# Hybrid decoder layer: another order of the output product's pieces, and a later place for one weight split

## The chip, the cores and the metric

The kernel runs on one core of one Trainium2 chip. The metric is the device time of one execution in microseconds (us); for the kernel before the change it is 1205.36 us, the median of 3 runs (1204.99 to 1206.16).

Engine names are those of the profile: PE (matrix products; PEld is its weight load), DVE (elementwise), ACT (activation functions, copies), POOL and SP (here they only issue transfers). Each engine has one queue of instructions, whose order is fixed when the program is built.

## What is computed

One decoder layer over 512 tokens of width 1024, in float32: a SwiGLU feed-forward block (ffn1), a mixer that joins dilated attention and a gated recurrence, and a second SwiGLU block (ffn2). The change lies where the mixer ends and ffn2 begins:

```python
merged = gates[:, :, 0] * attn_d + gates[:, :, 1] * rec_d
h = h + rms_norm(merged @ w_out[l], mix_norm_post[l])

f = swiglu(rms_norm(h, ffn2_norm_pre[l]), ffn2_w_gate[l], ffn2_w_up[l], ffn2_w_down[l])
h = h + 0.5 * rms_norm(f, ffn2_norm_post[l])
```

## The kernel before

**Number format.** A product of two float32 matrices is made of three: each operand is split into a high part (a copy rounded to the format that PE takes, made by ACT) and a low part (the rest, a subtraction on DVE). `split` (L317, L318) does it for weights; they come from memory over SP's queue into four `raw` buffers (L254), and a buffer is free again when the subtraction has read it. Lines L446 to L448 and L330 to L332 are the three products, high by high, high by low, low by high.

**Tokens in blocks.** The 512 tokens are four blocks of 128. `merged @ w_out` has rows = tokens and 1024 columns, taken as two halves of 512. The half of the contraction that comes first (`merged` columns 0 to 511) is done ahead of the change with a scheme of seven block products; its sums for every block and half lie in `facc`. The other half of the contraction is done by `out_product` (L537) in **eight pieces**, one for each (half, block): four steps over the contraction, three products each, twelve products of 128x512. Its weights are the four tiles `wo[0]` to `wo[3]`: the first two for half 0, the last two for half 1, two contraction steps in each. They are split by `other(0)` to `other(3)`, and the last of them is the only one named `wo` in the profile; the other three are named `act`.

**A piece** begins with a seed: ACT copies the earlier sum from `facc` into one of five PSUM accumulators (`begin`, L545). PE adds the twelve products. ACT squares the result and sums the squares along the row (`square`, L439, into `sq`); DVE multiplies by the norm's gain into `facc` (L554). A seed of a later piece waits until the accumulator of five pieces earlier has been read by L554.

**A block** is closed by `Boundary.block` behind the piece with its half 1. It needs the sums of squares of both halves. `root` (L426 to L433) makes the norm's factor in five small DVE steps with one ACT step (L428) between; DVE then adds the scaled block to the residual `h` (L572, two halves), ACT squares `h` (L439), POOL sends `h` to memory (`kept`, L574), a second `root` follows for the norm that ffn2 begins with, and DVE makes `u` (L579, two halves). The two `u` of a block are held until `Boundary.turn` takes them.

**A turn** transposes a block for ffn2: for each half four PE transposes into one of three `aux` PSUM buffers (L588), ACT's copy of the high part (L592), DVE's low part (L593) into `xf`, and ACT's copy of the whole into `facc` (L594).

**What follows.** `gemm_first` does the first five weight matrices of ffn2, first for tokens 0 to 255 (blocks 0 and 1), then for 256 to 511, with products of 128x256 (L330 to L332). Blocks 2 and 3 are turned behind the third and fourth matrix of the first round. Four of the five weight matrices have ordinary buffers (`w`); the fifth goes into `tx`. Its split is traced inside `issue_after` of two instructions named by `bd2.done[1]`: on ACT and on DVE it is queued behind them.

**Order.** The kernel's text gives a priority: what is written earlier goes first, unless it is not ready by the builder's estimate; `high_priority(offset)` moves instructions up (AHEAD for weight splits, EVAC for `root`). The builder writes out each engine's queue from that.

Of the kernel before, what the change touches and what calls it, by code (L numbers as in the profile page):

```python
# [10 lines left out]
F32 = mybir.dt.float32  # L11
F32R = mybir.dt.float32r
AF = mybir.ActivationFunctionType
ALU = mybir.AluOpType
# [172 lines left out]
def hybrid_layer(ctx: ExitStack, tc: tile.TileContext, xT: bass.AP, xN: bass.AP, wst: bass.AP,  # L187
                 first: bass.AP, rows: bass.AP, consts: bass.AP, bias: bass.AP, out: bass.AP):
    nc = tc.nc
    DVE, ACT, PE = nc.vector, nc.scalar, nc.tensor  # L190
# [25 lines left out]
    def hb(b, sl=slice(0, D)):  # L216

        return hs["t"][b // 2].rearrange("p k t -> p (k t)")[:, b % 2 * D:b % 2 * D + D][:, sl]

    def fb(b, sl=slice(0, D)):  # L220
        return facc[:, 2 * b:2 * b + 2, :].rearrange("p k t -> p (k t)")[:, sl]
# [14 lines left out]
    state = {"g": 0, "i": 0, "off": 0, "raw": None, "ahead": AHEAD, "split": None}  # L236
# [83 lines left out]
    def acc_ps():  # L320
        return psum.tile([P, T], F32, name="acc", tag="acc", bufs=5)

    def aux_ps():
        return psum.tile([P, T], F32, name="aux", tag="aux", bufs=3)

    def tmp(name):
        return tpool.tile([P, T], F32, name=name, tag="t")
# [84 lines left out]
    def stat():  # L412
        return tpool.tile([P, 1], F32, name="stat", tag="stat", bufs=24)

    def root(sums, f, then=lambda: None):


        *firsts, last = sums
        c = -0.5 * f / D
        with tc.high_priority(offset=EVAC):  # L420
            s0, bias_, y, v, r = (stat() for _ in range(5))
            s = firsts[0]
            if len(firsts) > 1:
                s = stat()
                DVE.tensor_add(s, *firsts)
            DVE.tensor_scalar(bias_, s, 1.0 / D, EPS, op0=ALU.mult, op1=ALU.add)  # L426
            DVE.tensor_scalar(s0, s, D * EPS, c, op0=ALU.add, op1=ALU.mult)
            ACT.activation(y, last, AF.Abs_reciprocal_sqrt, bias=bias_, scale=1.0 / D)  # L428
            with_last = DVE.scalar_tensor_tensor(v, last, c, s0, op0=ALU.mult, op1=ALU.add).ins
            with tc.issue_after(with_last):  # L430
                then()
            DVE.scalar_tensor_tensor(v, v, y, y, op0=ALU.mult, op1=ALU.mult)
            DVE.scalar_tensor_tensor(r, v, 1.5 * f, y, op0=ALU.add, op1=ALU.mult)  # L433
        return r

    def square(src):

        q, t = tmp("sq"), stat()
        state["square"] = ACT.activation(q[:, :src.shape[-1]], src, AF.Square, accum_out=t).ins  # L439
        return t  # L440

    def tokens(ps, ws, x, b, fill=lambda: None, ks=None, cs=slice(0, T), seeded=False):
        bl = slice(b * P, (b + 1) * P)
        for k in ks or range(x.n):
            wh, wl = (w.rearrange("p (k c) -> p k c", k=2)[:, k % 2, cs] for w in ws[k // 2])
            PE.matmul(ps, x.hi[k][:, bl], wh, start=k == 0 and not seeded, stop=False, skip_group_check=True)  # L446
            PE.matmul(ps, x.hi[k][:, bl], wl, start=False, stop=False, skip_group_check=True)  # L447
            PE.matmul(ps, x.lo[k][:, bl], wh, start=False, stop=k == x.n - 1, skip_group_check=True)  # L448
            if k == x.n // 2 - 1:
                fill()  # L450
# [7 lines left out]
    FHALVES = (slice(0, T), slice(T, D))  # L458

    def gains(pool, *ids):  # L460
# [5 lines left out]
        return t[:, 0, :], t[:, 1, :]  # L466

    def last_product(key, nk, x, added, grow, slots, block, fills={}, apart=False):


# [23 lines left out]
        def out_of(ps, b, cs, z=None):  # L494
            src, y = ps, fb(b, cs)
            if added and not apart:
                DVE.tensor_add(y, src, y)
                src = y
            sums.setdefault(b, []).append(square(src))
            return lambda: DVE.tensor_mul(z if z is not None else y, src, grow[:, cs])  # L500
# [3 lines left out]
        for half, fs in enumerate(FHALVES):  # L504
# [7 lines left out]
            for b in range(4):  # L512
                z, rest, ahead = tmp("z") if apart and half else None, [], None
                for i, (_, _, cs) in enumerate(pieces):
                    if pieces[i][:2] != (half, b):
                        continue
                    ps = next_of(i)
                    if not late or b > 1:
                        tokens(ps, ws, x, b, fills.get((half, b), lambda: None), cs=cs, seeded=apart)
                    with tc.issue_after(ahead) if ahead else nullcontext():  # L520
                        rest.append(out_of(ps, b, slice(fs.start + cs.start, fs.start + cs.stop),
                                           z if z is None else z[:, cs]))
                    if cs.stop == LAST:
                        ahead = rest.pop()().ins
                if ahead:

                    block(b, sums[b], z, rest.pop())
                    continue
                for f in rest:
                    f()  # L530
                if half:
                    block(b, sums[b], *([z] if apart else []))
                elif b == 1:

                    warm(sums[1][0])

    def out_product(ws, x, grow, bd):  # L537

        order = [(half, 2 * h + k) for h in range(2) for half in range(2) for k in range(2)]
        begun, sums = [], {}  # L540

        def begin():
            half, b = order[len(begun)]
            begun.append(acc_ps())
            ACT.activation(begun[-1], fb(b, FHALVES[half]), AF.Copy)  # L545

        begin()
        for i, (half, b) in enumerate(order):
            if len(begun) < 8:
                begin()  # L550
            ps, fs = begun[i], FHALVES[half]
            tokens(ps, ws[half], x, b, (lambda: bd.turn(0)) if i == 6 else (lambda: None), seeded=True)
            sums.setdefault(b, []).append(square(ps))
            DVE.tensor_mul(fb(b, fs), ps, grow[:, fs])  # L554
            if half:
                bd.block(b, sums[b])
            if i == 6:
                bd.turn(1)

    class Boundary:  # L560

# [6 lines left out]
        def block(self, b, sums):  # L568
            r = root(sums, self.f)
            sums = []  # L570
            for fs in FHALVES:
                DVE.scalar_tensor_tensor(hb(b, fs), fb(b, fs), r, hb(b, fs), op0=ALU.mult, op1=ALU.add)  # L572
                sums.append(square(hb(b, fs)))
            nc.gpsimd.dma_start(self.kept[b], hb(b))  # L574
            r = root(sums, 1.0)
            us = []
            for fs in FHALVES:
                u = tmp("u")
                last = DVE.scalar_tensor_tensor(u, hb(b, fs), r, self.grow[:, fs], op0=ALU.mult, op1=ALU.mult)  # L579
                us.append(u)  # L580
            self.u[b] = us
            self.done[b] = state["square"], last.ins

        def turn(self, b):
            for i, u in enumerate(self.u.pop(b)):
                ps = aux_ps()
                for j in range(4):
                    PE.transpose(ps[:, j * P:(j + 1) * P], u[:, j * P:(j + 1) * P], ident)  # L588
                for ks, *two in self.parts(i):
                    src = ps.rearrange("p (k t) -> p k t", k=4)[:, ks]  # L590
                    hi, lo = (t[:, :, b * P:(b + 1) * P] for t in two)
                    ACT.activation(hi, src, AF.Copy)  # L592
                    DVE.tensor_sub(lo, src, hi.bitcast(F32))  # L593
                ACT.activation(fb(b, FHALVES[i]), ps, AF.Copy)  # L594

    class Form:

# [603 lines left out]
    for k in range(KC):  # L1201
        wh, wl, raw = wts[k]
        if k == 0:
# [3 lines left out]
            for sl in HALVES:  # L1207
                tail = ACT.activation(wh[:, sl], raw[:, sl], AF.Copy).ins
            DVE.scalar_tensor_tensor(u1.lo[0], z, col("g1a", 0), u1.hi[0].bitcast(F32),
                                     op0=ALU.mult, op1=ALU.subtract)  # L1210
# [69 lines left out]
    with ExitStack() as mx:  # L1280
# [38 lines left out]
        def values_two(steps, then):  # L1319
# [78 lines left out]
            for j in range(2):  # L1398
# [4 lines left out]
        t, steps = forms_of(lambda i, j: Form(lambda s, k: um_t[2 * i + k // 2][:, s, k % 2, HALVES[j]]),  # L1403
                            apool, False, rec_half)
        values_first()
        pairs = [[(g * 4 + hd, 12 + g * 4 + hd) for g in range(NG)] for hd in range(NH)]
        order = [("pair",) + p for ps in pairs for p in ps] + [("pair", 52 + c, 53 + c) for c in range(0, KC, 2)]
# [165 lines left out]
        for c in range(0, KC, 2):  # L1573
            g, u = tmp("g"), tmp("u")
# [5 lines left out]
        for c in range(KC):  # L1580
            ps = acc_ps()
# [5 lines left out]
    with ExitStack() as mx:  # L1587
# [181 lines left out]
        xs, ws = {}, {}  # L1769
# [7 lines left out]
        q = sig[:, 0:4, :].rearrange("p (i j) (h t) -> p i h j t", i=2, h=2)  # L1777
# [28 lines left out]
        for c in range(KC):  # L1806
            if c < 3:
                ps = pss[c]
            else:
                ps = acc_ps()  # L1810
# [19 lines left out]
    ws = {}  # L1830
# [39 lines left out]
    b = [aux_ps() for _ in range(2)]  # L1870
# [33 lines left out]
    with tc.high_priority(offset=EVAC):  # L1904
        for dst, ps in zip(at(1, 0), z):
            DVE.tensor_add(dst, ps, dst)
    other(3)
    out_product([wo[:2], wo[2:]], mg, grow3, bd2)
    keys = [(w, 2, i) for i in range(NSTD[2]) for w in ("gate", "up")]
    pss = gemm_first(keys[:NFIRST], u2, [spare(ap2)["tx"]],  # L1910
# [145 lines left out]
```

## Time and profile before

| | |
|---|---|
| median of 3 runs | 1205.36 us |
| the profiled execution, its own time | 1204.48 us |
| its span, first to last instruction | 1202.7 us |
| mean granted clock of PE | 0.999 |
| PE idle in the span | 9.7 us |
| `out_product`, first L446 to the first L330 of ffn2 | 833.57 to 858.96 us |

Times in the profile are counted from the span's start. A row of a timeline gives start, duration, engine, line, operation, what is written and read, how many were merged, and in brackets how long the engine had been idle before it and what ended the wait. Matrix products are pipelined, so a row's duration is longer than the distance to the next start; the distance is what a product costs in a stream.

### The profile page before, as it was taken

Reading aid. Unit: us, or ns where it says so; the run is one execution under the profiler, and the core shown is the slowest. Engines: PE = TensorE matmul, PEld = TensorE weight load, DVE = VectorE, ACT = ScalarE, POOL = GpSimd, SP = SyncE. Lnnn points to the kernel's source line nnn. Section 1 sums busy time; section 2 is a strip of 40 time slices with the busy share of each in tenths; the row PEclk is TensorE's granted clock in tenths of the full one; section 3 lists DMA queues with packets and bytes.
Section 4 is the critical chain, followed back from the end, with each engine's and each line's share of the span. In section 5 each row is a group of like instructions: output and inputs, shape, how many; then the busy total and the mean of one; then the engine's idle time right before and its main releaser. Section 6 shows DMA issues by size and latency. Waiting matters only on the chain.

```text
span 1202.7 us, 18558 instructions
## 1 busy us (share of the span) xinstructions
PE 1193.0 (99%) x7042; PEld 1058.2 (88%) x7042; DVE 1060.1 (88%) x1675; ACT 853.8 (71%) x1484; POOL 26.1 (2%) x51
## 2 busy tenths in 40 slices
PE   9999999999999999999999999999999999999997
PEld 8899999999888889888888888888899889899996
DVE  7999888989689999999978899888899898989964
ACT  7566787887566676777836988747666788888763
POOL 0000000000011000000000000000100000000000
PEclk9999999999999999999999999999999999999999
DMA  7223333434625222222323432226543333433341
GB/s 268 88 101 131 121 140 107 140 114 151 248 104 163 71 97 88 97 83 85 108 71 120 168 114 103 78 81 209 176 141 124 105 141 105 141 105 141 123 158 71
DMA packets 45818, 149.75 MB, mean 125 GB/s; under 512 B 5152, under 2 KB 8608, under 8 KB 45728
## 3 DMA queue, kind: packets, MB, share of 16 engines
q1 hardware_dynamic: 38160, 131.09, 31.7%
q0 software_dynamic: 7280, 17.30, 4.2%
q8 instruction: 55, 0.90, 0.3%
q14 instruction: 35, 0.29, 0.1%
q10 hardware_dynamic: 288, 0.17, 0.0%
HBM read 138.06 MB, written 6.29 MB: 120 GB/s over the span
## 4 chain that ended last, share of the span: by engine, by line
PE 93%; DVE 3%; ACT 3%; issue 1%; DMA 0%; DVEq 0%
PE acc L829 13%; PE acc L779 8%; PE acc L781 8%; PE acc L780 8%; PE acc L332 7%; PE acc L331 7%; PE acc L330 7%; PE acc L832 7%; PE aux L1114 4%; PE aux L1115 4%; PE aux L1116 4%; PE aux L448 1%; PE aux L447 1%; PE aux L446 1%; ACT w L317 1%
## 5 line engine op out<-in xcount | busy, mean ns | idle before, releaser
L318 DVE TENSOR_TENSOR w<-raw,w 128x1024 fp32r<-128x1024 f32 (+1 forms) x274 | 299.0, 1097 | 38.0 <-ACT w L317 37.4
L317 ACT ACTIVATE w<-raw 128x1024 fp32r<-128x1024 f32 (+1 forms) x274 | 261.2, 958 | 79.8 <-PE acc L332 35.5
L779 PE MATMUL acc<-big,w 128*128 128x256 f32 x716 | 203.0, 284 | 0.0
L781 PE MATMUL acc<-big,w 128*128 128x256 f32 x716 | 202.6, 283 | 0.0
L780 PE MATMUL acc<-big,w 128*128 128x256 f32 x716 | 202.6, 283 | 0.0
L829 PE MATMUL acc<-big,w 128*128 128x512 f32 x524 | 144.2, 395 | 0.1
L779 PEld LDWEIGHTS acc<-big,w 128*128 128x128 f32 x716 | 137.2, 192 | 1.4
L780 PEld LDWEIGHTS acc<-big,w 128*128 128x128 f32 x716 | 137.2, 192 | 1.2
L781 PEld LDWEIGHTS acc<-big,w 128*128 128x128 f32 x716 | 137.2, 192 | 0.0
L829 PEld LDWEIGHTS acc<-big,w 128*128 128x128 f32 x524 | 89.9, 188 | 12.2 <-PE acc L832 0.2
L832 PEld LDWEIGHTS acc<-big,w 128*128 128x128 f32 x524 | 80.2, 188 | 10.8
L1114 PE MATMUL aux<-w,xf 128*128 128x512 f32 x224 | 87.5, 391 | 0.0
L1115 PE MATMUL aux<-w,xf 128*128 128x512 f32 x224 | 87.5, 391 | 0.0
L1116 PE MATMUL aux<-w,xf 128*128 128x512 f32 x224 | 87.2, 389 | 0.0
L832 PE MATMUL acc<-big,w 128*128 128x256 f32 x524 | 84.5, 281 | 0.0
L318 DVE TENSOR_TENSOR w<-s,w 128x1024 fp32r<-128x1024 f32 x51 | 62.1, 1217 | 2.7 <-ACT w L317 2.5
L331 PE MATMUL acc<-xf,w 128*128 128x512 f32 (+1 forms) x168 | 58.7, 350 | 0.3 <-DVE xf L593 0.3
L317 ACT ACTIVATE w<-s 128x1024 fp32r<-128x1024 f32 x51 | 53.8, 1055 | 7.2 <-PE acc L781 3.8
L332 PE MATMUL acc<-xf,w 128*128 128x512 f32 (+1 forms) x168 | 58.6, 349 | 0.0
L330 PE MATMUL acc<-xf,w 128*128 128x512 f32 (+1 forms) x168 | 58.5, 351 | 0.0
L837 ACT ACTIVATE acc<-acc 128x512 f32<-128x512 f32 x75 | 44.2, 589 | 13.5 <-PE acc L832 11.7
L1116 PEld LDWEIGHTS aux<-w,xf 128*128 128x128 f32 x224 | 42.1, 188 | 8.9
(510 smaller groups left out, 2903.5 us busy)
## 6 DMA issues: line engine op xcount, KB each, us to landing
raw<-in_w SPq DMA_DIRECT2D x232, 512.0 KB, 3.3
big<-xf POOLq DMA_DIRECT2D x6, 512.0 KB, 3.2
gains<-in_rows POOLq DMA_DIRECT2D x5, 512.0 KB, 5.4
h<-in_x SPq DMA_DIRECT2D x8, 256.0 KB, 5.1
h<-in_xn POOLq DMA_DIRECT2D x4, 512.0 KB, 5.8
kept_m<-h POOLq DMA_DIRECT2D x4, 512.0 KB, 2.9
vals<-in_w SPq DMA_DIRECT2D x4, 512.0 KB, 6.4
h<-kept_m POOLq DMA_DIRECT2D x4, 512.0 KB, 5.4
```

The costliest lines, as they stand in the source:

```text
L317: state["split"] = ACT.activation(dh, src, AF.Copy).ins
L318: state["low"] = DVE.tensor_sub(dl, src, dh.bitcast(F32)).ins
L330: PE.matmul(ps, wh, xh, start=first, stop=False)
L331: PE.matmul(ps, wh, xl, start=False, stop=False)
L332: PE.matmul(ps, wl, xh, start=False, stop=last)
L779: PE.matmul(ps, wh, xh, start=start and k == 0, stop=False, skip_group_check=True)
L780: PE.matmul(ps, wh, xl, start=False, stop=False, skip_group_check=True)
L781: state["product"] = PE.matmul(ps, wl, xh, start=False, stop=k == 3, skip_group_check=True).ins
L829: PE.matmul(part, w[p][:, 0, ks[k]], at(BOTH, k), start=start and k == 0, stop=False, skip_group_check=True)
L832: last = PE.matmul(cross, w[p][:, 1, ks[k]], at(0, k), start=False, stop=k == 3, skip_group_check=True)
L1114: PE.matmul(ps, xh, wh, start=first and j == 0, stop=False, skip_group_check=True)
L1116: PE.matmul(ps, xl, wh, start=False, stop=j == 1, skip_group_check=True)
```

## The change

The eight pieces come in another order. Before, they go by pairs of blocks, half by half; after, both halves of block 0 come first, then both of block 1, then blocks 2 and 3 as before:

| piece | 1 | 2 | 3 | 4 | 5 | 6 | 7 | 8 |
|---|---|---|---|---|---|---|---|---|
| before (half, block) | 0,0 | 0,1 | 1,0 | 1,1 | 0,2 | 0,3 | 1,2 | 1,3 |
| after | 0,0 | 1,0 | 0,1 | 1,1 | 0,2 | 0,3 | 1,2 | 1,3 |

Block 0 is turned behind the fifth piece, before in the middle of the seventh; block 1 behind the seventh, as before. `done[b]`, behind which the fifth weights are split for b = 1, was block 1's last square of `h` on ACT and the last L579 on DVE; now it is the last L594 and the last L593 of block 1's turn.

```diff
     def square(src):
 
         q, t = tmp("sq"), stat()
-        state["square"] = ACT.activation(q[:, :src.shape[-1]], src, AF.Square, accum_out=t).ins
+        ACT.activation(q[:, :src.shape[-1]], src, AF.Square, accum_out=t)
         return t
...
     def out_product(ws, x, grow, bd):
 
-        order = [(half, 2 * h + k) for h in range(2) for half in range(2) for k in range(2)]
+        order = [(0, 0), (1, 0), (0, 1), (1, 1), (0, 2), (0, 3), (1, 2), (1, 3)]
+        turns = {4: 0, 6: 1}
         begun, sums = [], {}
...
-            tokens(ps, ws[half], x, b, (lambda: bd.turn(0)) if i == 6 else (lambda: None), seeded=True)
+            tokens(ps, ws[half], x, b, seeded=True)
             sums.setdefault(b, []).append(square(ps))
             DVE.tensor_mul(fb(b, fs), ps, grow[:, fs])
             if half:
                 bd.block(b, sums[b])
-            if i == 6:
-                bd.turn(1)
+            if i in turns:
+                bd.turn(turns[i])
...
-                last = DVE.scalar_tensor_tensor(u, hb(b, fs), r, self.grow[:, fs], op0=ALU.mult, op1=ALU.mult)
+                DVE.scalar_tensor_tensor(u, hb(b, fs), r, self.grow[:, fs], op0=ALU.mult, op1=ALU.mult)
                 us.append(u)
             self.u[b] = us
-            self.done[b] = state["square"], last.ins
...
                     ACT.activation(hi, src, AF.Copy)
-                    DVE.tensor_sub(lo, src, hi.bitcast(F32))
-                ACT.activation(fb(b, FHALVES[i]), ps, AF.Copy)
+                    low = DVE.tensor_sub(lo, src, hi.bitcast(F32)).ins
+                self.done[b] = ACT.activation(fb(b, FHALVES[i]), ps, AF.Copy).ins, low
```

## The prediction

> **What bounds the kernel now.** I read the page first, then the waits of PE, then PE's timeline around the change, and last the timelines of DVE and ACT over the same stretch. First the engine shares, then the largest of PE's waits on work.
>
> ```profile
> span 1202.7 us, 18558 instructions
> ...
> PE 1193.0 (99%) x7042; PEld 1058.2 (88%) x7042; DVE 1060.1 (88%) x1675; ACT 853.8 (71%) x1484; POOL 26.1 (2%) x51
> ```
>
> ```profile
> PE aux L588 <- DVE u L579: 1.8, 2, 1.6
> ```
>
> PE is idle for 1202.7 - 1193.0 = 9.7 us in all, so a reordering can win little; the longest single wait (1.6 us) is that of block 1's transposes (L588) for u (L579), and it lies inside the function that changes. Its stretch on PE, start and duration in us:
>
> ```profile
> 833.57 0.39 PE L446 MATMUL acc<-act,big 128*128 128x512 f32 x1
> ...
> 844.45 0.39 PE L446 MATMUL acc<-act,big 128*128 128x512 f32 x1
> ...
> 851.25 1.03 PE L588 MATMUL aux<-cst,u 128*128 128x128 f32 x8
> 852.04 0.48 PE L446 MATMUL acc<-wo,big 128*128 128x512 f32 x1
> 852.36 0.40 PE L447 MATMUL acc<-wo,big 128*128 128x512 f32 x1
> ...
> 853.50 0.39 PE L446 MATMUL acc<-act,big 128*128 128x512 f32 x1
> 855.47 0.66 PE L588 MATMUL aux<-cst,u 128*128 128x128 f32 x4 [1.57 <-DVE u L579]
> ...
> 857.60 0.60 PE L588 MATMUL aux<-cst,u 128*128 128x128 f32 x4
> ...
> 858.96 0.73 PE L330 MATMUL acc<-xf,w 128*128 128x256 f32 x4
> 860.03 0.38 PE L331 MATMUL acc<-xf,w 128*128 128x256 f32 x1 [0.34 <-DVE xf L593]
> ...
> 860.38 0.28 PE L330 MATMUL acc<-xf,w 128*128 128x256 f32 x1
> ...
> 860.61 0.28 PE L332 MATMUL acc<-xf,w 128*128 128x256 f32 x1
> ```
>
> From 833.57 to 844.45 four pieces of twelve products run without a gap: 10.88 / 48 = 0.227 us each, 2.72 us a piece. Eight transposes take 852.04 - 851.25 = 0.79 us, and the product behind them costs 0.32 instead of 0.227, so a block's turn is about 0.88 us. Eight pieces and two turns without a wait would need 8 x 2.72 + 2 x 0.88 = 23.5 us and end at 857.1. The first product of the next stage (L330) starts at 858.96: **1.9 us lost**. That stage then needs six products before 860.38; at (860.61 - 860.38) / 2 = 0.115 us each they would end 0.69 after 858.96, at 859.65: **0.7 us more lost**, to the low halves of block 1 (L593). So 2.6 us is everything that a better order can win here.
>
> Why u of block 1 is late, on DVE:
>
> ```profile
> 839.90 0.68 DVE L554 TENSOR_TENSOR facc<-acc,gains 128x512 f32<-128x512 f32 x1
> 840.50 1.22 DVE L318 TENSOR_TENSOR w<-raw,w 128x1024 fp32r<-128x1024 f32 x1
> 841.85 0.69 DVE L554 TENSOR_TENSOR facc<-acc,gains 128x512 f32<-128x512 f32 x1
> ...
> 843.82 0.69 DVE L554 TENSOR_TENSOR facc<-acc,gains 128x512 f32<-128x512 f32 x1 [1.15 <-ACT sq L439]
> ...
> 848.12 1.41 DVE L579 SCALAR_TENSOR_TENSOR u<-h,stat,gains 128x512 f32<-128x512 f32 x2
> ...
> 849.57 0.68 DVE L554 TENSOR_TENSOR facc<-acc,gains 128x512 f32<-128x512 f32 x1
> ...
> 854.21 0.22 DVE L432 SCALAR_TENSOR_TENSOR stat<-stat 128x1 f32<-128x1 f32 x1 [0.98 <-ACT stat L428]
> ...
> 854.66 1.41 DVE L579 SCALAR_TENSOR_TENSOR u<-h,stat,gains 128x512 f32<-128x512 f32 x2
> 855.99 0.68 DVE L593 TENSOR_TENSOR xf<-aux,xf 128x512 fp32r<-128x512 f32 x1
> ...
> 860.57 1.40 DVE L572 SCALAR_TENSOR_TENSOR h<-facc,stat,h 128x512 f32<-128x512 f32 x2
> 861.89 1.21 DVE L318 TENSOR_TENSOR tx<-raw,tx 128x1024 fp32r<-128x1024 f32 x1
> ...
> 869.79 1.42 DVE L579 SCALAR_TENSOR_TENSOR u<-h,stat,gains 128x512 f32<-128x512 f32 x2
> ```
>
> A block's chain is about 5.7 us of alternating DVE and ACT steps from its last L554 to the end of its u (843.82 to 849.53), and the chains stand one behind another: block 1's last L554 (849.57) starts when block 0's u is done, though its products were over at about 844.6 (the fifth piece starts at 844.45). Block 1's chain takes 6.5 us (849.57 to 856.07), 0.8 more, and ACT shows with what:
>
> ```profile
> 831.10 1.06 ACT L317 ACTIVATE wo<-raw 128x1024 fp32r<-128x1024 f32 x1 [0.24 <-DMA raw<-in_w]
> ...
> 841.15 0.58 ACT L439 ACTIVATE sq<-acc 128x512 f32<-128x512 f32 x1
> ...
> 843.11 0.58 ACT L439 ACTIVATE sq<-acc 128x512 f32<-128x512 f32 x1
> ...
> 851.65 0.63 ACT L439 ACTIVATE sq<-h 128x512 f32<-128x512 f32 x1 [1.67 <-DVE h L572]
> ...
> 852.95 1.04 ACT L317 ACTIVATE tx<-raw 128x1024 fp32r<-128x1024 f32 x1
> 853.90 0.28 ACT L428 ACTIVATE stat<-stat 128x1 f32<-128x1 f32 x1
> 854.08 0.57 ACT L592 ACTIVATE xf<-aux 128x512 fp32r<-128x512 f32 x1
> ```
>
> The split of the fifth weights (tx, 1.04 us) stands ahead of block 1's root (L428, 853.90), and DVE's L432 waits 0.98 for it. Block 0's copies (L592) come behind all that, though its transposes ended at about 852.3.
>
> **The change part by part.** *The new order* gives block 0 its second half one piece earlier. The square of the second piece starts at 841.15, that of the third at 843.11; block 0's chain starts with the former in place of the latter, 1.96 us earlier: less than a piece (2.72), because the squares queue behind weight splits and seeds. Nothing is added: the same eight pieces, squares, seeds and transposes. The second piece now reads the wo weights from its seventh product on, at 833.57 + 18 x 0.227 = 837.65; they are split on ACT at 831.10 and on DVE directly behind (1.23 us), over by 833.5, so this costs nothing with 4 us to spare, and their transfer is unmoved.
>
> *Turn 0* moves on PE from 851.25 to behind the fifth piece, 833.57 + 5 x 2.72 = 847.17. Block 0's u starts at 848.12 - 1.96 = 846.16, its halves end at 846.9 and 847.6: the second half is met within 0.1 to 0.3 us. Bounds: if the chain does not move (849.5), PE waits 2.3 us; if it moves by the full piece, nothing. I take 0.2. A gap of 2 to 3 us raises the question of PE's clock; the columns of this row, a stretch that holds the wait of 1.57 us, end with granted clock, DMA share and GB/s:
>
> ```profile
> 850.00:855.50 5.50, 3.93 (x23) 3.01 (x21) 3.71 (x13) 3.85 (x10) 0.54 (x1) 1.00 0.23 95
> ```
>
> The clock stays at 1.00, so I price waits by their length alone. [...]
>
> *Block 1's chain.* Its last L554 can run directly behind block 0's u and its own first half: 847.6 + 0.6 = 848.2, instead of 849.57: 1.4 us earlier. The split of tx is gone from its way: 0.8. So its u would end at 856.07 - 2.2 = 853.9. Against that, block 0's two L593 (0.68 each) may now fall into it: 0 to 1.4 us, partly in gaps such as the 0.98 above; I take 0.5, so u is there by 853.8 (first half) and 854.4. PE comes to turn 1 behind the seventh piece at 833.57 + 7 x 2.72 + 0.88 + 0.2 = 853.7. A wait of 0.1 for the first half and 0.3 for the second; bounds 0 and 1.3; I take 0.5.
>
> *The end of the stage.* The last piece covers 2.72 us behind turn 1, while copy and subtraction need 0.57 + 0.68 a half, and two of the four L593 are no longer queued there. I take 0.2 (bounds 0 and 0.7, what it costs now).
>
> *The fifth weights.* Their split, 1.04 on ACT and 1.21 on DVE, moves behind block 1's last copy, into block 2's chain; nothing new is computed. Behind it on ACT stand block 2's squares and root, and for these DVE waits. PE reads tx here:
>
> ```profile
> 872.02 1.12 PE L588 MATMUL aux<-cst,u 128*128 128x128 f32 x8
> 872.90 0.37 PE L330 MATMUL acc<-xf,tx 128*128 128x256 f32 x1
> ```
>
> so the product itself has 9 us. What is late next is block 3's turn at 872.02: its u ends at 869.79 + 1.42 = 871.2, only 0.8 ahead. If PE comes 1.7 earlier, u must be 0.9 earlier. DVE reaches block 2's h at 860.57; without two L593 (1.3) and with u of block 1 over 1.6 earlier it can do so 2 to 2.9 earlier; the moved split gives back up to 1.0. Left: 1.0 to 2.9 earlier, enough; I take nothing. The two DMA queues that the moved steps touch, SP's refill of the raw buffer that tx frees and POOL's copy of block 0's h to memory:
>
> ```profile
> 863.17 0.33 SPq L254 DMA_DIRECT2D raw<-in_w  x1
> 882.18 0.33 SPq L254 DMA_DIRECT2D raw<-in_w  x1
> ```
>
> ```profile
> 847.00 0.54 POOL L574 DMA_DIRECT2D kept<-h  x1 [23.96 <-DVE stat L427]
> ```
>
> SP has nothing to issue for 19 us behind that refill, so some us later delay no other transfer; POOL has been idle for 24 us ahead of the copy, which moves up with block 0's chain and meets nothing. I take nothing for either.
>
> Sum: 0.2 + 0.5 + 0.2 = 0.9 us of waits left of 2.6: **1.7 us won**. Made against the profiled execution, 1204.48 us (span 1202.7 and 1.8 around it), it gives 1202.8; that execution is 0.9 under the median, 1205.36, which is what will be compared, so I forecast 1203.7 (1203.0 to 1204.9 if this case holds).
>
> **The rivals.** *All waits go.* Every bound at its good end: 2.6 won, 1202.8. For it: ACT stands idle for 1.67 us ahead of 851.65, where block 0's copies would go now, so they need cost nothing there. Against it: u of block 0 arrives within 0.4 us of its transposes, and block 3's u has 0.8 to give.
>
> *The stall only moves.* Block 0's evacuation, traced at an earlier place, stands on DVE and ACT ahead of block 1's root and waits there for PE. Then block 1's last L554 starts where it does now (847.17 + 0.79 for the transposes, 0.57 + 0.68 twice, give 850.5), its u at 855 to 856, and PE waits as before: 1205.4.
>
> *Slower: turn 0 is met too early.* The order of each engine is fixed when the program is built; the row at 855.47 shows that it places a turn up to 1.6 us ahead of its data. If block 0's chain keeps its place behind the weight splits (840.50, 1.22 us) and seeds, PE stands at 847.17 for 2.3 us; block 1's chain then runs as now with two L593 more, u at 857.4, where PE comes at 855.9: 1.5 more; its evacuation, 1.3 us behind that, still ends under the last piece. That is 3.8 of waits; the squares and L554s of the fifth and sixth pieces (0.69 each) in the same chain make it up to 5.2, the moved split in the next block's chain up to 6.2. Against the 2.6 of now 1.2 to 3.6 are lost, 2.4 in the middle: 1207.8. It decides from the point where block 0's u ends later than about 848.9, 1.7 behind its place on PE.
>
> **How the numbers follow.** The forecast 0.40, all waits gone 0.24, the stall only moves 0.08, slower 0.28. 0.2% is 2.4 us, about what a measurement of this kernel can tell from no change. Only the second case reaches it on the fast side (1202.8 against 1202.95), and barely, so 0.02 of it goes to no change: faster 0.22. Of the slower case half lies beyond 1207.77, 0.14, and I add 0.08, taken evenly from the other cases, for an order of the engines' queues that differs elsewhere too: slower 0.22. Same: 0.56. The range runs from all waits gone, less 0.4 for noise, 1202.4, to the middle of the slower case, 1207.8; beyond it lie the upper half of that case and little else.
>
> **What would show it.** Right, if the changed trace has eight L588 behind the fifth piece with under 0.5 us of idle; block 1's L588 behind the seventh with under 1 us; the first L330 about 25.4 - 1.2 = 24.2 us behind the stage's first L446 in place of 25.4; tx's L317 behind the last L594 of block 1; and block 3's L588 without idle. Wrong, if block 0's square of the second piece does not take the third's place on ACT, if an L593 waiting for PE stands ahead of block 1's root on DVE, or if a wait appears ahead of the transposes of blocks 2 or 3.

## The result and the profile after

The changed kernel takes 1203.74 us, the median of 22 executions (1202.85 to 1205.05); the kernel before, measured beside it, 1205.69 us (22 executions, 1204.18 to 1207.95). The ratio is 0.9984 with a 95% interval of 0.9978 to 0.9991: 1.9 us less, between 1.1 and 2.7. Measured twice more beside the kernel before, the same kernel gave 0.9980 and 0.9983. The forecast was 1203.7 us, with 1.7 us won.

The profiled execution took 1203.19 us, span 1201.4. First the head of the page of the changed kernel (the span and the busy time of the engines):

```profile
span 1201.4 us, 18560 instructions
...
PE 1193.2 (99%) x7042; PEld 1057.9 (88%) x7042; DVE 1060.0 (88%) x1675; ACT 854.7 (71%) x1484; POOL 26.1 (2%) x51
```

The work is the same, 7042 products and 1193 us of PE; what fell is PE's idle time, from 9.7 to 8.2 us. PE's timeline of the changed kernel around the change, columns as before (lines below L546 are one higher than before: L555 was L554, L573 was L572, L580 was L579; L588 to L594 are unchanged):

```profile
834.16 0.39 PE L446 MATMUL acc<-act,big 128*128 128x512 f32 x1
...
847.53 0.39 PE L448 MATMUL acc<-act,big 128*128 128x512 f32 x1
847.76 1.15 PE L588 MATMUL aux<-cst,u 128*128 128x128 f32 x8
848.67 0.48 PE L446 MATMUL acc<-act,big 128*128 128x512 f32 x1
...
854.01 0.39 PE L448 MATMUL acc<-wo,big 128*128 128x512 f32 x1
854.52 1.38 PE L588 MATMUL aux<-cst,u 128*128 128x128 f32 x8
855.65 0.48 PE L446 MATMUL acc<-act,big 128*128 128x512 f32 x1
...
858.50 0.28 PE L330 MATMUL acc<-xf,w 128*128 128x256 f32 x1
...
859.21 0.28 PE L330 MATMUL acc<-xf,w 128*128 128x256 f32 x1
...
870.88 1.04 PE L588 MATMUL aux<-cst,u 128*128 128x128 f32 x8
...
871.87 0.28 PE L331 MATMUL acc<-xf,tx 128*128 128x256 f32 x1
```

Turn 0 stands behind the fifth piece and keeps PE from its next product for 0.91 us where 0.79 is its own work: 0.12 lost. Turn 1 stands 0.28 later than the stream would put it (854.52 against 854.01 + 0.227) and holds PE for 1.13 in place of 0.79: some 0.6 lost. Behind it the low halves are there in time: the seventh 128x256 product stands 0.71 behind the first, about what six products cost. So 25.05 us pass from the first L446 to that seventh product, against 26.81 us before (833.57 to 860.38). The list of PE's waits, which before had 1.6 us for u and 0.3 for the low halves in this stretch, has none there now; the 0.6 at turn 1 hardly shows in it, because the modelled ends of the product rows cover most of it. On ACT of the changed kernel:

```profile
831.54 1.06 ACT L317 ACTIVATE wo<-raw 128x1024 fp32r<-128x1024 f32 x1 [0.20 <-DMA raw<-in_w]
...
841.77 0.58 ACT L439 ACTIVATE sq<-acc 128x512 f32<-128x512 f32 x1
...
851.37 0.58 ACT L592 ACTIVATE xf<-aux 128x512 fp32r<-128x512 f32 x1
...
852.46 0.59 ACT L594 ACTIVATE facc<-aux 128x512 f32<-128x512 f32 x1
852.93 0.29 ACT L428 ACTIVATE stat<-stat 128x1 f32<-128x1 f32 x1
853.12 0.59 ACT L594 ACTIVATE facc<-aux 128x512 f32<-128x512 f32 x1
...
857.74 1.33 ACT L594 ACTIVATE facc<-aux 128x512 f32<-128x512 f32 x2 [0.48 <-DVE xf L593]
858.97 1.05 ACT L317 ACTIVATE tx<-raw 128x1024 fp32r<-128x1024 f32 x1
```

The square of the second piece (841.77) is now the one that block 0's chain starts with. The split of the fifth weights now stands behind the last L594 of block 1, and in its former place ahead of block 1's root (L428) stands a copy of block 0 (L594). On DVE of the changed kernel:

```profile
846.78 1.42 DVE L580 SCALAR_TENSOR_TENSOR u<-h,stat,gains 128x512 f32<-128x512 f32 x2
...
848.90 0.69 DVE L555 TENSOR_TENSOR facc<-acc,gains 128x512 f32<-128x512 f32 x1
...
852.00 0.68 DVE L593 TENSOR_TENSOR xf<-aux,xf 128x512 fp32r<-128x512 f32 x1
...
853.26 0.22 DVE L432 SCALAR_TENSOR_TENSOR stat<-stat 128x1 f32<-128x1 f32 x1 [0.51 <-ACT stat L428]
...
853.71 1.42 DVE L580 SCALAR_TENSOR_TENSOR u<-h,stat,gains 128x512 f32<-128x512 f32 x2
...
867.96 1.42 DVE L580 SCALAR_TENSOR_TENSOR u<-h,stat,gains 128x512 f32<-128x512 f32 x2
```

**A clock that repeats.** Counted from the stage's first L446, three profiles of the changed kernel differ by 0.4 us. Counted from the start of the `wo` weights' split on ACT (831.54 above, 831.10 before), they agree: block 0's u starts 15.24, 15.25 and 15.24 us behind it, and the first L331 that reads tx 40.33, 40.35 and 40.32. Before, it is 848.12 - 831.10 = 17.02 and 873.11 - 831.10 = 42.01; the row of PE of the kernel before that gives the latter is

```profile
873.11 0.28 PE L331 MATMUL acc<-xf,tx 128*128 128x256 f32 x1
```

From there to the end of the span it is 329.4 to 329.6 us in every kernel below. So an execution here is the arrival of the `wo` weights, plus the stretch up to this L331, plus a constant: PE waits for the chain at its turns, and the chain counts from the weights. Where the weights come late, even the start of the stage does: in e11 below, with the weights 2 us later, the first L446 waits 0.74 us for its seed, which ACT copies behind their split. The stretch is 1.68 us shorter after the change. The profiled executions differ by only 1.3 us because the weights came 0.44 us later in the second. This stretch, called S below, is the measure of the experiments.

### The profile page after: what moved, and what is told of

It reads as the page before. It is cut to its first block, busy times and chain, and to the rows that moved or that the text cites. A ratio compares the mean times of both kernels' runs of the same rounds, so it can differ in the third digit from the quotient of the medians.

```text
span 1201.4 us, 18560 instructions
## 1 busy us (share of the span) xinstructions
PE 1193.2 (99%) x7042; PEld 1057.9 (88%) x7042; DVE 1060.0 (88%) x1675; ACT 854.7 (71%) x1484; POOL 26.1 (2%) x51
## 4 chain that ended last, share of the span: by engine, by line
PE 93%; DVE 3%; ACT 3%; issue 1%; DMA 1%; DVEq 0%
PE acc L829 13%; PE acc L779 8%; PE acc L781 8%; PE acc L780 8%; PE acc L330 7%; PE acc L332 7%; PE acc L331 7%; PE acc L832 7%; PE aux L1114 4%; PE aux L1115 4%; PE aux L1116 4%; PE aux L447 1%; PE aux L446 1%; PE aux L448 1%; ACT w L317 1%
## 5 line engine op out<-in xcount | busy, mean ns | idle before, releaser
L330 PE MATMUL acc<-xf,w 128*128 128x512 f32 (+1 forms) x168 | 59.0, 351 | 0.2 <-ACT w L1208 0.2
L331 PE MATMUL acc<-xf,w 128*128 128x512 f32 (+1 forms) x168 | 58.7, 349 | 0.0
```

Source lines behind the costliest of these rows:

```text
L330: PE.matmul(ps, wh, xh, start=first, stop=False)
L331: PE.matmul(ps, wh, xl, start=False, stop=False)
```

## The experiments

Theory: the order of the pieces moves the chains of blocks 0 and 1 forward, the turn of block 0 uses that, and the split leaves block 1's chain; the parts need one another. Rivals: the stall only moves; turn 0 met too early costs more than it brings; one part alone does it all. Each timed kernel was run 11 times beside 26 or 33 executions of the kernel before.

| kernel | new order | turn 0 behind piece 5 | split behind turn 1 | S, us | S minus before | time by before, 95% |
|---|---|---|---|---|---|---|
| before | | | | 42.01 | | 1 |
| changed | x | x | x | 40.33 | -1.68 | 0.9984 (0.9978 to 0.9991) |
| order alone | x | | | 41.56 | -0.45 | 0.9998 (0.9989 to 1.0007) |
| split alone | | | x | 41.43 | -0.58 | 0.9996 (0.9987 to 1.0005) |
| turn alone | | x | | 42.86 | +0.85 | 1.0005 (0.9996 to 1.0014) |
| order and turn | x | x | | 40.83 | -1.18 | 0.9989 (0.9980 to 0.9997) |
| order and split | x | | x | 40.56 | -1.45 | 0.9987 (0.9978 to 0.9995) |
| turn and split | | x | x | 41.37 | -0.64 | 0.9994 (0.9985 to 1.0003) |

S comes from one profiled execution, the ratio from all timed ones, and they agree within 0.25 us: 0.0001 of the ratio is 0.12 us. For the order alone the table has the second of two profiles; the first, with S 43.09, was hit by a slow clock (0.73 from 855 to 860, last section). The timings alone tell only those kernels of the table from before that have the new order and another part. The finer comparisons rest on S, which repeated within 0.03 us over three profiles of the changed kernel, and on the wait that each trace names; the other kernels have one undisturbed profile each.

**The order alone.**

```diff
-        order = [(half, 2 * h + k) for h in range(2) for half in range(2) for k in range(2)]
+        order = [(0, 0), (1, 0), (0, 1), (1, 1), (0, 2), (0, 3), (1, 2), (1, 3)]
```

> The new order of the pieces alone; turn 0 in the middle of the seventh piece and the fifth weights' split as before. Measure: the stage, from the first L446 of the eight pieces to the seventh 128x256 product behind them: 26.8 us before, 25.05 with the whole change. Theory (block 0's chain starts 1.9 us earlier and draws block 1's with it): block 0's u about 1.9 earlier, block 1's u about 1.3 earlier, the stage 25.9 (25.5 to 26.3): half of the gain, since the split still stands in block 1's chain. Rival (the place of turn 0 and of the split do it, the order is only cover): block 1's u not earlier by more than 0.3, the stage 26.6 to 27. Time against before: 0.9 less by the theory, none by the rival.

Measured: 1204.66 us, ratio 0.9998. The profiled execution, 1206.49 us, was the slowest of its eleven, so the same kernel was profiled once more, as e10:

> The new order alone, once more, for its profile: turn 0 in the middle of the seventh piece, turn 1 behind it, fifth weights' split where it was. Theory (the longer product spacing behind turn 1 in the first profile of this kernel was a chance event of that one execution): the products behind block 1's transposes are 0.227 us apart again, the granted clock stays at 1.00 in every stretch of the stage, the first product that reads the fifth weights stands about 39.1 us behind the stage's first L446, and the execution takes about 1204.9 us. Rival (it comes from the two waits of 0.52 and 1.23 us around block 1's transposes whenever these occur): the waits are there again and the products behind them are about 0.43 us apart for some 3 us, 40.7 us to the first such product, about 1206.4 us. In both, the second half of block 1's transposes waits over 0.8 us for block 0's copy on ACT (L594).

PE's waits in e10, from its list of waits (what PE waited for: us in total, times, longest):

```profile
PE aux L588 <- ACT facc L594: 1.2, 1, 1.2
PE aux L588 <- DVE u L579: 0.5, 1, 0.5
```

Block 0's u comes 1.76 us earlier (15.26 against 17.02 behind the weights), block 1's 1.35, and the wait for it shrinks from 1.57 to 0.5. But a new wait of 1.2 takes its place: there are three `aux` buffers, block 0's turn holds two of them until its L594 has read them, and its turn still stands in the seventh piece. So the fourth half cannot be transposed before ACT has copied the first. The theory is right on the chains and wrong on the stage: 26.64 us in e10 in place of 25.9, which is the rival's 26.6 to 27. In large part this is "the stall only moves", by a resource that the prediction did not name. e10 took 1204.61 us beside 1206.08 of before, one execution each; its products ran at full speed (granted clock 1.00 from 833 to 880) and S is 41.56, as its theory had it. What befell the first profile is told under the hardware.

**The split alone.**

```diff
-            self.done[b] = state["square"], last.ins
...
-                    DVE.tensor_sub(lo, src, hi.bitcast(F32))
-                ACT.activation(fb(b, FHALVES[i]), ps, AF.Copy)
+                    low = DVE.tensor_sub(lo, src, hi.bitcast(F32)).ins
+                self.done[b] = ACT.activation(fb(b, FHALVES[i]), ps, AF.Copy).ins, low
```

> Only the fifth weights' split is moved behind block 1's turn; old order, old turns. Theory (the split of 1.04 us on ACT costs block 1's chain 0.8): block 1's root on ACT no longer waits, its u 0.8 earlier, the stage 26.0 (25.8 to 26.3) in place of 26.8. Rival (other ACT work takes its place, a copy L592 of block 0): u not earlier by more than 0.3 and the stage 26.6 to 26.9. Second rival (the split in block 2's chain makes block 3's turn late): a wait ahead of block 3's L588, which only 0.8 us of slack covered, and the time back to that of before.

Measured: 1204.84 us, ratio 0.9996. Block 1's u starts 22.75 behind the weights, 0.81 earlier; the wait for it falls from 1.57 to 1.10, and 0.29 for the `aux` buffer appears. PE's rows of e2 at its turn 1:

```profile
854.94 0.66 PE L588 MATMUL aux<-cst,u 128*128 128x128 f32 x4 [1.10 <-DVE u L579]
...
856.83 0.66 PE L588 MATMUL aux<-cst,u 128*128 128x128 f32 x4 [0.29 <-ACT facc L594]
```

Block 3's u comes 0.8 later (39.49 behind the weights, 38.69 before), since the split now lies in the later chains; block 3's turn then falls on both sides of the first tx product, and PE takes 1.38 us from the product ahead of it to the first L331 with tx, 1.11 in the changed kernel. The stage, 26.28 us to the seventh product, is as the theory had it.

**The turn alone.**

```diff
+        turns = {4: 0, 6: 1}
...
-            tokens(ps, ws[half], x, b, (lambda: bd.turn(0)) if i == 6 else (lambda: None), seeded=True)
+            tokens(ps, ws[half], x, b, seeded=True)
...
-            if i == 6:
-                bd.turn(1)
+            if i in turns:
+                bd.turn(turns[i])
```

> Only turn 0 is moved, to behind the fifth piece; old order, old split. Theory (turn 0 is then met before block 0's u is done, and its copies stand in block 1's chain): PE waits 1.2 to 1.8 us at turn 0, block 1's u 0.5 to 1.4 later than before relative to the stage's start, the stage 27.3 to 28.5, slower by 0.5 to 1.7 us. Rival (an early turn is what wins, since it takes block 0's copies out of the crowd behind block 1's chain): the stage 26.3 or less.

Measured: 1205.99 us, ratio 1.0005, S 0.85 longer. PE's timeline of e3 at both turns and at the start of ffn2:

```profile
847.31 0.39 PE L446 MATMUL acc<-act,big 128*128 128x512 f32 x1
849.12 0.66 PE L588 MATMUL aux<-cst,u 128*128 128x128 f32 x4 [1.42 <-DVE u L579]
...
856.70 1.24 PE L588 MATMUL aux<-cst,u 128*128 128x128 f32 x8
...
859.74 0.39 PE L330 MATMUL acc<-xf,w 128*128 128x256 f32 x1 [0.18 <-DVE facc L554]
...
861.14 0.39 PE L331 MATMUL acc<-xf,w 128*128 128x256 f32 x1 [0.28 <-DVE xf L593]
```

This is the mechanism of the prediction's slower rival: block 0's chain keeps its place and PE meets turn 0 too early. It shows as a wait of 1.42, and block 1's u is 0.90 later behind the weights (24.46 against 23.56). The price is lower than the 1.2 to 3.6 us that the rival had. One more product stands ahead of the transposes than behind five pieces, and they wait only for the first half of u. And the 1.57 of turn 1 is nearly gone in turn (1.00 us from the transposes to the next product at 857.70, of which 0.79 is their work), because the builder put this turn half a piece later, behind the sixth product of the last piece. That is paid for behind it: the first products of ffn2 wait for DVE three times, 0.18, 0.34 and 0.28.

**Order and turn.** Both diffs above, the split left where it was.

> The new order and the new turns, the fifth weights' split as before behind block 1's last square. Theory (order and split add up): block 1's u 0.5 to 0.9 later than with the whole change, the stage 25.6 to 26.0 in place of 25.05. Rival (with the new turns the split finds a gap on ACT and its place does not matter): the stage 25.0 to 25.3 and the time that of the whole change.

Measured: 1203.73 us, ratio 0.9989, S -1.18. The turn, which costs 0.85 with the old order, brings 0.73 with the new one. The split does not hurt block 1's u here (22.16 behind the weights, as in the changed kernel), because its place in ACT's queue is now behind the root. It hurts the end of the stage: DVE's rows of e4,

```profile
855.76 1.22 DVE L318 TENSOR_TENSOR tx<-raw,tx 128x1024 fp32r<-128x1024 f32 x1
...
859.01 0.68 DVE L593 TENSOR_TENSOR xf<-aux,xf 128x512 fp32r<-128x512 f32 x1
...
859.67 0.68 DVE L593 TENSOR_TENSOR xf<-aux,xf 128x512 fp32r<-128x512 f32 x1
```

show block 1's subtractions behind it. PE waits for one (0.23 by its row), and the seventh 128x256 product stands 1.20 behind the first in place of 0.71. With the split moved, S is 0.50 shorter. So the stage came as long as the theory had it (25.94 us for 25.6 to 26.0), but not by its way, a later u of block 1.

**Order and split.** The changed kernel with turn 0 back in the middle of the seventh piece.

```diff
-        turns = {4: 0, 6: 1}
...
-            tokens(ps, ws[half], x, b, seeded=True)
+            tokens(ps, ws[half], x, b, (lambda: bd.turn(0)) if i == 6 else (lambda: None), seeded=True)
...
-            if i in turns:
-                bd.turn(turns[i])
+            if i == 6:
+                bd.turn(1)
```

> The new order and the moved split, turn 0 still in the middle of the seventh piece. Theory (block 0's late evacuation holds the PSUM buffers and crowds ACT and DVE behind block 1's chain): block 1's u at 18.7 to 19.2 us from the stage's start, earlier than with the whole change (19.55), but the second half of its transposes waits 1 us or more for a copy of block 0 (L594), and the stage to the first tx product is 38.0 to 39.0, against 37.5 with the whole change and 39.3 before. Rival (turn 0's place costs nothing): 37.5 or less.

Measured: 1204.01 us, ratio 0.9987; the changed kernel measured beside it, 1203.15. PE's row of e6:

```profile
857.36 0.66 PE L588 MATMUL aux<-cst,u 128*128 128x128 f32 x4 [0.86 <-ACT facc L594]
```

Block 1's u is the earliest of all, 21.39 behind the weights, 0.8 ahead of the changed kernel's, since nothing of turn 0 lies in its chain. It is of no use: the fourth half waits 0.86 for an `aux` buffer, a little less than the 1 us of the theory. The early turn of block 0 is worth 0.23 in S by freeing these buffers, although it puts its own copies into block 1's chain.

**Turn and split.** The changed kernel with the old order line.

> The two other parts without the new order: turn 0 behind the fifth piece, fifth weights' split behind block 1's transposes, pieces in the old order. Theory (the order is what makes the two other parts worth anything; without it turn 0 is met too early whatever the split does): turn 0 waits about 1.4 us for block 0's u as with the moved turn alone, block 1's turn has no long wait, because the evacuation of block 0 is over by then and the split no longer stands in block 1's chain; first product of the fifth weights 39.2 to 39.8 us behind the stage's first L446, 1205.0 to 1205.7 us beside 1205.5 of before. Rival (the parts simply add: -0.4 for the split and +0.7 for the turn, each in us of the medians with the other parts absent): the same time within the interval, so the two theories differ from a third, that the split alone carries the turn: under 1204.3 us and no wait of over 0.5 us at turn 0.

Measured: 1204.63 us, ratio 0.9994, S -0.64; its profiled execution, 1205.78 us, had the weights 2 us later than before (833.07). Turn 0 waits 1.47 and turn 1 has no wait, as the theory had it, yet the whole is faster than it allowed: with the split gone, turn 1 costs nothing, which pays for turn 0's wait. In S the parts do not add: -0.58 and +0.85 would make +0.27; the times alone (0.9985 to 1.0003) could not tell. The theory holds for the turn, which brings next to nothing in S on top of the split alone (0.06) and 0.23 on top of order and split. It falls for the split, which is worth 0.58 by itself and 1.49 on top of the turn. The order has the largest share in the whole: 1.04 on top of the two others.

**Block 0's copies behind the root.** The 0.51 of idle time ahead of DVE's L432 at 853.26 in the changed kernel suggests a further gain: issue block 0's L594 behind block 1's root.

```diff
+                with tc.issue_after(state["root"]) if self.late and b == 0 else nullcontext():
+                    self.done[b] = ACT.activation(fb(b, FHALVES[i]), ps, AF.Copy).ins, low
```

> The whole change, and block 0's two copies into facc (L594) queued on ACT behind block 1's second root (L428), which they precede in the changed trace. Theory (what is left of the wait at turn 1 is block 0's evacuation inside block 1's chain): ACT reaches L428 0.4 to 0.5 us earlier, block 1's u 0.4 to 0.5 earlier, the stage to the first tx product 37.1 in place of 37.5 us. Rival (the third PSUM buffer decides, which these copies set free for the second half of turn 1): the second half of block 1's transposes waits for L594 by 0.5 or more and the stage is 37.5 to 38.2.

Measured: 1203.56 us, ratio 0.9982 (0.9973 to 0.9991). The mechanism works: block 1's u starts 21.84 behind the weights, 0.33 ahead of the changed kernel's, a little less than the theory had, and S is 40.01, 0.32 shorter; turn 1 has no wait for L594, so the rival falls. In time it cannot be told from the changed kernel (0.9980 beside it, 0.9971 to 0.9989), so it is no proven improvement.

> The whole change once more, as the comparison for the others of this call. Theory: 1.4 to 2.4 us less than before, the stage to the first tx product 37.3 to 38.2 us. If block 0's chain starts with a transfer that lands a little earlier or later in each execution, its u lies at 12.6 to 13.0 us from the stage's start and the waits at the turns move by as much; if not, all positions repeat within 0.1.

This was the changed kernel unedited, beside e5 and e6: 1203.15 us, ratio 0.9980 (0.9971 to 0.9989).

**The gains later.** The chain counts from the weights, and two copies of gains, 0.5 MB each, are issued by POOL while they are loaded (from 822.48 on in the changed kernel, 5.6 us to landing). e8 is the changed kernel with these two issued by SP behind the last of the weights that the stage reads.

```diff
-    grow3, grow4 = gains(ap2, 2, 3)
+    grow34 = ap2.tile([P, 2, D], F32, name="gains", tag="wd", bufs=1)
+    grow3, grow4 = grow34[:, 0, :], grow34[:, 1, :]
...
+    with tc.issue_after(state["load"]), tc.high_priority(offset=AHEAD):
+        for j in range(2):
+            nc.sync.dma_start(grow34[:, j, :], bass.AP(tensor=rows.tensor, offset=rows.offset + (2 + j) * D,
+                                                       ap=[[0, P], [1, D]]))
```

> The whole change, and the two transfers of the gains (0.5 MB each), which POOL issues while the output weights are on their way, are issued by SP behind the last of the output weights. Theory (ACT waits 2.3 us for the third output weights because the gains share the DMA engines, and the squares of block 0 queue behind that): the wait of L317 for raw shrinks by 1 us or more, block 0's u lies at 12.0 or less from the stage's start in place of 12.6, the waits at turns 0 and 1 shrink from 0.8 to 0.3, the stage to the first tx product is 37.0 to 37.3. Rival (the weights wait for their raw buffer, not for bandwidth): L317 waits as before. Second rival (the gains land too late): L555 waits for gains and the stage is longer than 38.

Measured: 1203.91 us, ratio 0.9986, S 41.50; no gain. ACT's rows of e8:

```profile
828.71 1.06 ACT L317 ACTIVATE act<-raw 128x1024 fp32r<-128x1024 f32 x1 [0.55 <-DMA raw<-in_w]
831.62 1.06 ACT L317 ACTIVATE wo<-raw 128x1024 fp32r<-128x1024 f32 x1 [1.85 <-DMA raw<-in_w]
...
836.85 1.06 ACT L317 ACTIVATE w<-raw 128x1024 fp32r<-128x1024 f32 x1 [1.00 <-DMA raw<-in_w]
```

The `act` weights come 1.6 us earlier than in the changed kernel, the `wo` weights do not, and now a later weight is late, 1.00 at 836.85, probably because SP has the gains ahead of its later loads, which no row here shows. ACT's waits for the third and fourth weights, 2.34 and 0.20 in the changed kernel, are 0.55 and 1.85, so the wait moves from one to the next. The theory falls; of the rivals the first, in which the waits stay, comes nearest. Block 0's u starts 16.41 behind the weights in place of 15.24, and PE waits 0.70 at turn 0.

**Turn 1 later.** Most of what PE still loses is at turn 1, so e12 puts it in the middle of the last piece.

```diff
-        turns = {4: 0, 6: 1}
+        turns = {4: 0}
...
-            tokens(ps, ws[half], x, b, seeded=True)
+            tokens(ps, ws[half], x, b, (lambda: bd.turn(1)) if i == 7 else (lambda: None), seeded=True)
```

> The changed kernel with block 1's turn in the middle of the last piece (behind its sixth product) in place of behind the seventh piece. Theory (0.65 us of what PE still loses is turn 1, met 0.3 us ahead of u's first half and 0.34 more ahead of its second; the last piece's other half, 1.36 us, still covers block 1's copies): the turn takes 0.79 us without idle time, the first L330 stands 23.7 to 24.0 us behind the stage's first L446 in place of 24.3 to 24.8, and the time is 0.4 to 0.7 us under the changed kernel's of the same call. Rival (the cover is then too short: copy and subtraction of two halves take up to 2 x 0.68 + 0.58 = 1.9 us behind the transposes, and the next stage's products with block 1 wait for its low halves): a wait of 0.4 to 0.8 us at an L330, L331 or L332 for L593, and the same time as the changed kernel within 0.3 us.

> The changed kernel once more, beside the two others of this call. Both theories: 1203.0 to 1203.9 us, turn 0 1.15 to 1.32 us long and turn 1 1.38 us as in its other two profiles.

Measured: e12 1204.47 us, ratio 0.9993; e13, the changed kernel, 1203.36 and 0.9983. e12's turn takes 0.79 without a wait and the first L330 stands 23.79 behind the stage's start, as the theory had it. Then PE's rows and DVE's rows of e12:

```profile
857.40 0.62 PE L330 MATMUL acc<-xf,w 128*128 128x256 f32 x4
859.27 0.38 PE L331 MATMUL acc<-xf,w 128*128 128x256 f32 x1 [1.25 <-DVE stat L426]
```

```profile
857.20 1.41 DVE L573 SCALAR_TENSOR_TENSOR h<-facc,stat,h 128x512 f32<-128x512 f32 x2
858.53 0.68 DVE L593 TENSOR_TENSOR xf<-aux,xf 128x512 fp32r<-128x512 f32 x1
```

The rival holds, at a higher price than it named: 1.25 in place of 0.4 to 0.8. The row names L426, which follows on DVE directly behind the L593 of 858.53 (done at 859.21). Block 1's subtractions fell behind block 2's h in DVE's queue, where a turn half a piece earlier has them ahead of it. S is 41.20, 0.87 worse than the changed kernel's, and the time is 1.1 us longer.

## Why the prediction was right

The mechanism and the sum were right: 1.7 us won by the forecast, 1.68 in S, 1.9 (1.1 to 2.7) in time. That 1203.7 meets 1203.74 so closely is luck: the kernel before, from whose 1205.36 the forecast was made, measured 1205.69 over more executions, and the terms below are each a little off and cancel.

- **Block 0's chain**, 1.96 us earlier by the forecast, is 1.78 earlier behind the weights. The square of the second piece did take the place of the third's. That no transfer moves was right too, but the forecast placed the chain on PE's clock. It counts from the arrival of `wo`, and so it shifts from one execution to the next against PE.
- **Turn 0**: 0.2 of wait forecast, 0.12 measured; with the weights 0.4 us later against PE, as in the other two profiles of the changed kernel, its transposes take 1.32 in place of 1.15 and some 0.3 is lost; the first L330 then stands 24.75 and 24.72 us behind the stage's start, 24.34 in the first profile and 24.2 by the forecast.
- **Block 1's chain**: forecast were 1.4 earlier at its last L554, 0.8 for the split gone and 0.5 given back to block 0's evacuation, together 1.7. Its u is 23.56 - 22.17 = 1.39 earlier, and pairs of kernels take this apart. The order alone gives 1.35 (e10), 1.10 at the last L554 and 0.25 because a step of the root now stands ahead of it. The split gone gives 0.82 (e6 against e10), and 0.81 with the old order (e2): the forecast's 0.8. The early turn takes back 0.78 (22.17 against 21.39 in e6), not 0.5. The forecast laid this on the two L593, and they cost next to nothing: DVE waits 0.51 for ACT behind them (853.26). What costs is two copies on ACT, the L592 at 851.37 ahead of the second square of `h` and the L594 at 852.46 ahead of the root; e5 moves L594 and gets 0.33 back.
- **Turn 1**: 0.5 forecast, 0.6 measured. Of the signs of being wrong, one came near: two L593 do stand ahead of block 1's root on DVE, but DVE does not idle ahead of either. **The end of the stage**: 0.2 forecast, nothing measured.
- **The fifth weights' split at its new place**: nothing forecast, nothing measured. Block 3's u ends at 869.4, 1.5 ahead of its turn at 870.88, and none of the later turns waits. With the split alone it is late: in e2 block 3's u ends at 872.29, and PE starts its turn at 871.77.
- **The rivals.** All waits gone would have left 24.2 us to the seventh product; it is 25.05. PE meets turn 0 too early only with the old order (e3, e11), and only e3 is longer for it. "The stall only moves" has some truth that the forecast missed: whether it does hangs on three `aux` buffers. With the new order alone PE waits 1.2 for them, with order and split 0.86; only the early turn removes that wait. The forecast counted this turn as a risk and not as what sets the buffers free, and so had no term for its main use.

## What to carry to other kernels

Before moving a stall, list what the waiting instruction needs: its operand and its output buffer. Here, with the order alone, the operand's wait fell from 1.57 to 0.5 and the buffer's rose from nothing to 1.2. Look for the event from which a chain's times repeat from one execution to the next (here a transfer's arrival) and measure from it: a difference of 0.3 us showed there that the whole time, uncertain by a good 1 us, could not show. And a turn has two neighbours on each engine's queue: half a piece later it cost PE nothing itself and lost 1.25 us behind the next block's work.

## What the runs showed of the hardware

The first profile of the order alone lost 1.5 us more than the second (S 43.09 and 41.56) with the same waits at the same places. PE's rows of the first, e1:

```profile
854.20 0.40 PE L448 MATMUL acc<-wo,big 128*128 128x512 f32 x1
855.11 0.66 PE L588 MATMUL aux<-cst,u 128*128 128x128 f32 x4 [0.52 <-DVE u L579]
857.00 0.86 PE L588 MATMUL aux<-cst,u 128*128 128x128 f32 x4 [1.23 <-ACT facc L594]
857.51 0.77 PE L446 MATMUL acc<-act,big 128*128 128x512 f32 x1
858.09 0.63 PE L447 MATMUL acc<-act,big 128*128 128x512 f32 x1
...
860.65 0.43 PE L447 MATMUL acc<-wo,big 128*128 128x512 f32 x1
```

and of the second, e10:

```profile
853.85 0.39 PE L448 MATMUL acc<-wo,big 128*128 128x512 f32 x1
854.78 0.66 PE L588 MATMUL aux<-cst,u 128*128 128x128 f32 x4 [0.54 <-DVE u L579]
856.68 0.66 PE L588 MATMUL aux<-cst,u 128*128 128x128 f32 x4 [1.24 <-ACT facc L594]
857.09 0.49 PE L446 MATMUL acc<-act,big 128*128 128x512 f32 x1
```

A stretch of each, e1 and then e10; the last three columns are the granted clock, the DMA share and GB/s:

```profile
855.00:860.00 5.00, 3.65 (x14) 2.93 (x15) 4.93 (x13) 4.11 (x11) 0.76 (x1) 0.73 0.00 0
```

```profile
855.00:860.00 5.00, 3.76 (x21) 2.99 (x20) 4.93 (x13) 3.93 (x11) 0.77 (x1) 1.00 0.00 0
```

In e1 the products behind turn 1 are 0.43 us apart for 3.1 us (857.51 to 860.65), about half speed, and then 0.23 to 0.26 again. Its granted clock is 0.73 from 855 to 860, 0.93 from 860 to 865 and 1.00 from 833 to 855 and from 865 to 880. In e10 it is 1.00 throughout from 833 to 880, as it is around the turns (851 to 862) in the kernel before, the three profiles of the changed kernel, e4, e11 and e12. No single wait is over 1.24 us. But from one product to the next, with only eight transposes between, it is 3.31 us in e1 and 3.24 in e10, against 2.38 in the kernel before (853.50 to 855.88).

Why one of two nearly equal gaps was followed by a slow stretch and the other was not, these two profiles do not show, nor whether the gap had to do with it. The prediction had seen a clock of 1.00 around a wait of 1.57 us and priced waits by their length alone; in e1 two waits, of 0.52 and 1.23 us, and the transposes between them fell together, and the 1.5 us of the slow stretch came on top of them.

Two of the eleven timed executions of this kernel stood above 1206.3 us, the profiled one among them (mean granted clock 0.997), the others between 1203.9 and 1205.4. Whether the second had such a stretch was not profiled: its mean granted clock is 0.998, that of the nine others 0.999, but 0.998 also occurs in quick executions of other kernels (1202.87 us of the changed kernel).
